# Linear attention on one core: sixteen heads per transfer, Q in 8 KB runs, and features computed one group ahead

## The chip, the cores and the metric

One core of one Trainium2 chip. The metric is the device time of one launch in microseconds. Ratios are the mean time of one kernel's fast runs over that of the other's of the same rounds, so they are not quite the ratio of the medians that are quoted beside them. "Span" is the profiled execution's own length; the timed figure of the same execution lies 1.7 to 2.0 us above it.

## The reference

```python
batch, heads, seq, dim = 8, 12, 512, 64          # Q, K, V: float32
Q_feat = np.maximum(0, Q) + 1
K_feat = np.maximum(0, K) + 1
KV = np.einsum('bhkd,bhkv->bhdv', K_feat, V)
K_sum = np.sum(K_feat, axis=2)
numerator = np.einsum('bhqd,bhdv->bhqv', Q_feat, KV)
denominator = np.einsum('bhqd,bhd->bhq', Q_feat, K_sum)
return numerator / (denominator[:, :, :, None] + 1e-10)
```

Each of Q, K, V and the output is 12.58 MB. There are 96 heads. The kernel handles them in twelve groups (0 to 11) of eight heads; two groups make a pair (0 to 5).

## The kernel before

Loads cast float32 to bf16 on the way and are issued by GpSimd (only the first K comes uncast, over SyncE). VectorE computes features, copies three quarters of V into a block layout and divides the outputs; ScalarE copies the last quarter of V, the transposed Q and the K·V matrices. TensorE does transposes, first matmuls (K·V) and output matmuls; the program keeps TensorE's results in PSUM tiles and all other tiles in the SBUF. The page's GB/s count a load after its cast: GpSimd's queue moved 28.84 MB, 10.49 of stores and 18.35 of loads, which is half of the 36.70 MB that these loads read.

```python
    def load(s, groups, names="kvq"):            # s: a pair
        ...
            nc.gpsimd.dma_start(
                out=t[:, ms], in_=drams[x][:, 2 * groups[0] : 2 * groups[-1] + 2]
            )                                    # rows of 16 x 64 floats: 4 KB runs
    def store(g):
        o_sb = outs.pop(g)
        o_to = o_dram[:, g * NP : g * NP + NP]
        if g < NG - 2:
            nc.gpsimd.dma_start(out=o_to, in_=o_sb)          # 1 MB
            return
        for h in range(2):
            nc.sync.dma_start(out=o_to[:, h:NP:2], in_=o_sb[:, h:NP:2])   # 512 KB
    def v_blocks(g):
        ...                                      # block 3 by nc.scalar.copy, 0 to 2 by nc.vector.tensor_copy
    def transposes(g):
        qf = qfs.pop(g)
        qt = mid_pool.tile([P, C, P, 2], BF16, name="qt")
        for half in range(2):
            qt_ps = psum_qt.tile([P, C, P], BF16, name="qt_ps")     # two buffers
            for c in range(C):
                nc.tensor.transpose(qt_ps[:, c, :], qf[:, half * C + c, :, :], identity)
            nc.scalar.copy(out=qt[:, :, :, half], in_=qt_ps)
        qts[g] = qt
    ...
        for g in range(NG - 1):
            k_features(g); v_blocks(g); q_features(g)     # joined on a line here
            if g:
                transposes(g - 1)
            if g >= 2:
                output(g - 2)
            keys_values(g)
            if g % 2 and g // 2 + 2 < NG // 2:
                load_pair(g // 2 + 2)
            if g >= LAG:
                store(g - LAG)                            # LAG = 3
        last = NG - 1
        k_features(last); v_blocks(last)
        transposes(last - 1)
        output(last - 2)
        q_features(last)
        keys_values(last)
        transposes(last)
        output(last - 1)
        output(last)
        for g in range(last - LAG, NG):
            store(g)
```

Of the kernel before, what the change touches and what calls it, by code (L numbers as in the profile page):

```python
# [8 lines left out]
FP32 = mybir.dt.float32  # L9
BF16 = mybir.dt.bfloat16  # L10
# [1 line left out]

BANK = 512
IN_BUFS = 2
OUT_BUFS = 6
LAG = 3


@with_exitstack
def kernel(  # L20
# [15 lines left out]



    nc = tc.nc

    B, H, S, D = Q.shape
    P = 128
    C = 8
    C2 = 2 * C
    NPAIR = B * H * S // (P * C)
    NP = 4
    NG = NPAIR // NP
    D1 = D + 1
    W = 2 * D1

    def view(t, c):
        return t.flatten_outer_dims().rearrange("(n p c) d -> p n c d", p=P, c=c)

    q_dram = view(Q, C2)
    k_dram = view(K, C2)
    v_dram = view(V, C2)
    o_dram = view(out, C)

    const = ctx.enter_context(tc.tile_pool(name="const", bufs=1))
    head_pool = ctx.enter_context(tc.tile_pool(name="head_pool", bufs=1))  # L60
    in_pool = ctx.enter_context(tc.tile_pool(name="in_pool", bufs=IN_BUFS))
    feat_pool = ctx.enter_context(tc.tile_pool(name="feat", bufs=2))
    mid_pool = ctx.enter_context(tc.tile_pool(name="mid", bufs=3))
    out_pool = ctx.enter_context(tc.tile_pool(name="out_pool", bufs=OUT_BUFS))
    recip_pool = ctx.enter_context(tc.tile_pool(name="recip", bufs=4))
    psum_kva = ctx.enter_context(tc.tile_pool(name="psum_kva", bufs=2, space=bass.MemoryType.PSUM))
# [1 line left out]
    psum_qt = ctx.enter_context(tc.tile_pool(name="psum_qt", bufs=2, space=bass.MemoryType.PSUM))  # L68

    identity = const.tile([P, P], BF16, name="identity")  # L70
# [4 lines left out]
    zero = const.tile([P, 1], FP32, name="zero")  # L75
    kva_diag = [const.tile([P, 4, 2, D1], BF16, name=f"kva_diag{i}") for i in range(NV)]

    drams = dict(k=k_dram, v=v_dram, q=q_dram)
    raw = {}
    kfs = {}  # L80
    qfs = {}
    qts = {}
    outs = {}

    def own(g):
        return slice(g % 2 * 2, g % 2 * 2 + 2)

    def load_first_k():
        k_raw = head_pool.tile([P, 2, C2, D], FP32, name="k_first")
        nc.sync.dma_start(out=k_raw, in_=k_dram[:, 0:2])  # L90
        raw["k", 0] = k_raw

    def load(s, groups, names="kvq"):
        ms = slice(groups[0] % 2 * 2, groups[-1] % 2 * 2 + 2)
        for x in names:
            if (x, "buf", s) not in raw:
                raw[x, "buf", s] = in_pool.tile([P, 4, C2, D], BF16, name=f"{x}_raw")
            t = raw[x, "buf", s]
            nc.gpsimd.dma_start(  # L99
                out=t[:, ms], in_=drams[x][:, 2 * groups[0] : 2 * groups[-1] + 2]  # L100
            )
            for g in groups:
                raw[x, g] = t[:, own(g)]

    def load_pair(s):
        if s < NG // 2 - 1:
            load(s, (2 * s, 2 * s + 1))
        else:
            load(s, (2 * s,))
            load(s, (2 * s + 1,))  # L110

    def store(g):
        o_sb = outs.pop(g)
        o_to = o_dram[:, g * NP : g * NP + NP]
        if g < NG - 2:
            nc.gpsimd.dma_start(out=o_to, in_=o_sb)  # L116
            return
        for h in range(2):
            nc.sync.dma_start(out=o_to[:, h:NP:2], in_=o_sb[:, h:NP:2])

    def feature(dst, src):
        nc.vector.tensor_scalar(  # L122
            out=dst, in0=src, scalar1=1.0, scalar2=1.0, op0=ALU.add, op1=ALU.max
        )

    def k_features(g):
        k_raw = raw.pop(("k", g))
        kf = feat_pool.tile([P, C2, 2, D], BF16, name="kf")
        for n in range(2):
            feature(kf[:, :, n], k_raw[:, n])  # L130
        kfs[g] = kf

    def v_blocks(g):
        v_raw = raw.pop(("v", g))
        for b in range(4):
            ps = slice(32 * b, 32 * b + 32)
            if b == 3:
                nc.scalar.copy(out=v_blk[g % 2][ps, b], in_=v_raw[ps])  # L138
            else:
                nc.vector.tensor_copy(out=v_blk[g % 2][ps, b], in_=v_raw[ps])  # L140

    def q_features(g):
        q_raw = raw.pop(("q", g))
        qf = feat_pool.tile([P, C2, 2, D], BF16, name="qf")
        for half in range(2):
            cs = slice(half * C, half * C + C)
            feature(qf[:, cs].rearrange("p c n d -> p n c d"), q_raw[:, :, cs])
        qfs[g] = qf

    def keys_values(g):  # L150
        kf = kfs.pop(g)
        sb = g % 2
        vb = v_all[:, 4 * sb : 4 * sb + 5]
        kva_ps = psum_kva.tile([P, 5, D], FP32, name="kva_ps")
        for c in range(C2):
            for n in range(2):
                nc.tensor.matmul(  # L157
                    kva_ps[64 * n : 64 * n + 64],
                    lhsT=kf[:, c, n, :],
                    rhs=vb[:, :, n, c, :],  # L160
                    start=(c == 0),
                    stop=(c == C2 - 1),
                )
        kva = kva_diag[g % NV]
        for n in range(2):
            ps = slice(64 * n, 64 * n + 64)
            nc.scalar.copy(out=kva[ps, :, n, 0:D], in_=kva_ps[ps, sb : sb + 4, :])  # L167
            nc.scalar.copy(out=kva[ps, :, n, D], in_=kva_ps[ps, 4 - 4 * sb, 0:4])  # L168

    def transposes(g):  # L170
        qf = qfs.pop(g)
        qt = mid_pool.tile([P, C, P, 2], BF16, name="qt")
        for half in range(2):
            qt_ps = psum_qt.tile([P, C, P], BF16, name="qt_ps")
            for c in range(C):
                nc.tensor.transpose(qt_ps[:, c, :], qf[:, half * C + c, :, :], identity)  # L176
            nc.scalar.copy(out=qt[:, :, :, half], in_=qt_ps)  # L177
        qts[g] = qt

    def output(g):  # L180
        kva = kva_diag[g % NV]
        qt = qts.pop(g)
        o_sb = out_pool.tile([P, NP, C, D], FP32, name="o_sb")
        for h in range(2):
            ops = [psum.tile([P, 2, BANK], FP32, tag="ps", name="o_ps") for _ in range(2)]
            for c in range(C):
                for j in range(2):
                    b = 2 * h + j
                    nc.tensor.matmul(  # L189
                        ops[c // 4][64 * j : 64 * j + 64, c // 2 % 2, (c % 2) * W : (c % 2) * W + W],  # L190
                        lhsT=qt[:, c, 32 * b : 32 * b + 32, :],
                        rhs=kva[:, b],
                        start=True,
                        stop=True,
                    )
            for i in range(2):
                cells = ops[i][:, :, 0 : 2 * W].rearrange("p b (c n x) -> p b c n x", n=2, x=D1)
                recip = recip_pool.tile([P, 2, 2, 2, 1], FP32, name="recip")
                nc.vector.reciprocal(out=recip, in_=cells[:, :, :, :, D:D1])  # L199
                nc.vector.tensor_tensor(  # L200
                    out=o_sb[:, h:NP:2, 4 * i : 4 * i + 4].rearrange(
                        "p n (b c) d -> p b c n d", b=2
                    ),
                    in0=cells[:, :, :, :, 0:D],
                    in1=recip.to_broadcast([P, 2, 2, 2, D]),
                    op=ALU.mult,
                )
        outs[g] = o_sb

    def clear(first, split, end):  # L210
        t = v_all.rearrange("p b m c d -> p (b m c d)").bitcast(FP32)
# [5 lines left out]

    with tc.manual_schedule():
        nc.gpsimd.memset(zero, 0.0)
        load_first_k()  # L220
        load(0, (0,), "vq")
        load(0, (1,))
        nc.vector.memset(ones, 0.0)
        for b in range(4):
            nc.vector.memset(ones[32 * b : 32 * b + 32, b : b + 1], 1.0)  # L225
        clear(0, 3, 5)
        e = v_all[:, 4, :, :, 0:4].rearrange("p n c j -> p (n c) j")
        nc.vector.tensor_copy(out=e, in_=ones[:, None, :].to_broadcast([P, 2 * C2, 4]))
        make_identity(nc, identity)
        for t in kva_diag:  # L230
            nc.gpsimd.memset(t, 0.0)  # L231
        load_pair(1)
        clear(5, 7, 9)
        for g in range(NG - 1):
            k_features(g)
            v_blocks(g)
            q_features(g)
            if g:
                transposes(g - 1)
            if g >= 2:  # L240
                output(g - 2)
            keys_values(g)
            if g % 2 and g // 2 + 2 < NG // 2:
                load_pair(g // 2 + 2)
            if g >= LAG:
                store(g - LAG)
        last = NG - 1
        k_features(last)
        v_blocks(last)
        transposes(last - 1)  # L250
        output(last - 2)
        q_features(last)
        keys_values(last)
        transposes(last)
        output(last - 1)
        output(last)
        for g in range(last - LAG, NG):
            store(g)


# [28 lines left out]
```

## Time and profile before

| | before |
|---|---|
| time, median | 127.14 us of 3 runs; 127.23 of 4 with the run beside the changed kernel |
| span of the profiled run | 125.8 us |
| busy: VectorE (DVE), ScalarE (ACT), TensorE (PE) | 88.2, 68.0, 65.2 us |
| transfers over the span | 400 GB/s, read and written together |
| transfers, packets under 512 B | 38, 608 |

No compute engine is busy for more than about 70% of the span, while the DMA row of the page is 9 from end to end (the prediction shows it). So read the DMA row first, and ask of each stage whether the transfers were kept fed; the average shares of the engines cannot say that.

### The profile page before, as it was taken

What the parts mean: (1) busy time and instruction counts of PE and PEld (TensorE: products, weight loads), DVE (VectorE), ACT (ScalarE), POOL (GpSimd) and SP (SyncE); (2) the same over time, 40 slices, a digit from 0 to 9 for tenths busy, and PEclk for the clock granted to TensorE, in tenths of its full rate; (3) what the DMA queues carried; (4) which work ended last, traced back from release to release, by engine and by line L of the source; (5) the groups of instructions that cost most, each with busy time, mean ns of one, the idle gap of its engine ahead of it and who ended that gap; (6) DMA issues with size and microseconds to landing.
All of it is one profiled execution on the core that took longest, in us unless ns stands there. A gap on an engine that the chain in (4) does not pass through costs nothing.

```text
span 125.8 us, 2337 instructions
## 1 busy us (share of the span) xinstructions
PE 65.2 (52%) x960; PEld 48.4 (39%) x960; DVE 88.2 (70%) x188; ACT 68.0 (54%) x87; POOL 27.8 (22%) x43
## 2 busy tenths in 40 slices
PE   0005939000059784796918476006978569694500
PEld 0003627000036564574806365004656447472300
DVE  4896280206199799999989990629959999758920
ACT  7832296006700889629892962750087971987000
POOL 6990213000002082023700260212221002020000
PEclk9999999755555999689999999955589976999955
DMA  3999999999999999999999999999999999999991
GB/s 76 341 211 209 210 213 211 210 212 211 212 211 212 211 214 212 210 212 214 253 414 287 209 210 212 213 369 380 209 210 210 211 287 418 418 417 410 403 391 72
DMA packets 13419, 32.13 MB, mean 255 GB/s; under 512 B 608, under 2 KB 608, under 8 KB 13408
## 3 DMA queue, kind: packets, MB, share of 16 engines
q0 software_dynamic: 12048, 28.84, 98.3%
q1 hardware_dynamic: 1360, 3.15, 6.8%
q8 instruction: 7, 0.11, 0.3%
q14 instruction: 4, 0.03, 0.1%
HBM read 37.75 MB, written 12.58 MB: 400 GB/s over the span
## 4 chain that ended last, share of the span: by engine, by line
DMA 40%; DVE 26%; PE 18%; POOL 6%; issue 6%; DVEq 0%; POOLq 0%
DMA q_raw<-in_Q_dram 40%; DVE o_sb L200 15%; PE kva_ps L157 11%; DVE v_all L140 4%; PE qt_ps L176 3%; DVE recip L199 3%; PE o_ps L189 3%; POOL v_raw L99 2%; DVE qf L122 2%; DVE kf L122 2%; POOL q_raw L99 1%; POOL kva_diag L231 1%; POOL k_raw L99 1%; POOL identity masks.py:199 0%; POOL identity masks.py:197 0%
## 5 line engine op out<-in xcount | busy, mean ns | idle before, releaser
L157 PE MATMUL kva_ps<-v_all,kf 128*64 128x320 bf16 x384 | 36.4, 356 | 13.1 <-DVE v_all L140 13.1
L189 PE MATMUL o_ps<-kva_diag,qt 128*64 128x130 bf16 x384 | 19.1, 234 | 40.9 <-DVE o_sb L200 40.4
L200 DVE TENSOR_TENSOR o_sb<-o_ps,recip 128x512 f32<-128x512 f32 x48 | 33.2, 692 | 1.6
L140 DVE COPY v_all<-v_raw 32x2048 bf16<-32x2048 bf16 x36 | 26.5, 736 | 10.9 <-DMA v_raw<-in_V_dram 10.6
L157 PEld LDWEIGHTS <-kf 128*64 128x64 bf16 x384 | 25.3, 133 | 20.9 <-DVE v_all L140 13.3
L189 PEld LDWEIGHTS <-qt 128*64 128x64 bf16 x384 | 12.7, 114 | 46.4 <-DVE o_sb L200 44.6
L138 ACT COPY v_all<-v_raw 32x2048 bf16<-32x2048 bf16 x12 | 22.7, 1894 | 13.3 <-DMA v_raw<-in_V_dram 13.1
L177 ACT COPY qt<-qt_ps 128x1024 bf16<-128x1024 bf16 x24 | 29.7, 1308 | 0.3
L167 ACT CAST kva_diag<-kva_ps 64x256 bf16<-64x256 f32 x24 | 8.9, 371 | 33.3 <-PE kva_ps L157 33.2
L122 DVE TENSOR_SCALAR qf<-q_raw 128x1024 bf16<-128x1024 bf16 x24 | 9.1, 423 | 6.6 <-DMA q_raw<-in_Q_dram 6.5
L99 POOL DMA_DIRECT2D k_raw<-in_K_dram x7 | 5.3, 754 | 38.1 <-DVE kf L122 37.3
L116 POOL DMA_DIRECT2D out_dram<-o_sb x10 | 8.4, 846 | 22.6 <-DVE o_sb L200 16.4
L176 PE MATMUL qt_ps<-identity,qf 128*128 128x128 bf16 x192 | 13.1, 222 | 0.0
L199 DVE RECIPROCAL recip<-o_ps 128x8 f32<-128x8 f32 x48 | 9.6, 199 | 4.9 <-PE o_ps L189 4.8
L122 DVE TENSOR_SCALAR kf<-k_raw 128x1024 bf16<-128x1024 bf16 x22 | 8.7, 437 | 6.0 <-DMA k_raw<-in_K_dram 6.0
L176 PEld LDWEIGHTS <-qf 128*128 128x128 bf16 x192 | 11.0, 99 | 3.3 <-issue 3.0
L99 POOL DMA_DIRECT2D v_raw<-in_V_dram x8 | 6.1, 764 | 18.8 <-ACT v_all L138 10.7
L99 POOL DMA_DIRECT2D q_raw<-in_Q_dram x8 | 5.9, 741 | 4.2 <-DMA q_raw<-in_Q_dram 4.2
L213 DVE MEMSET v_all<- 128x3072 f32 (+1 forms) x2 | 4.4, 2192 | 1.1 <-DVE ones L225 0.7
L168 ACT CAST kva_diag<-kva_ps 64x4 bf16<-64x4 f32 x24 | 4.0, 169 | 0.0
L214 ACT COPY v_all<-zero 128x2048 f32<-128x2048 f32 x2 | 3.7, 1894 | 0.0
L214 ACT ACT_TABLE_LOAD x1 | 1.3, 1283 | 0.7 <-PEq L273 0.7
(12 smaller groups left out, 4.6 us busy)
## 6 DMA issues: line engine op xcount, KB each, us to landing
out_dram<-o_sb POOLq DMA_DIRECT2D x10, 1024.0 KB, 20.2
k_raw<-in_K_dram POOLq DMA_DIRECT2D x4, 1024.0 KB, 18.0
v_raw<-in_V_dram POOLq DMA_DIRECT2D x4, 1024.0 KB, 20.9
q_raw<-in_Q_dram POOLq DMA_DIRECT2D x4, 1024.0 KB, 25.0
v_raw<-in_V_dram POOLq DMA_DIRECT2D x4, 512.0 KB, 17.3
q_raw<-in_Q_dram POOLq DMA_DIRECT2D x4, 512.0 KB, 17.1
out_dram<-o_sb SPq DMA_DIRECT2D x4, 512.0 KB, 5.1
k_raw<-in_K_dram POOLq DMA_DIRECT2D x3, 512.0 KB, 23.3
```

Source lines behind the costliest of these rows:

```text
L99: nc.gpsimd.dma_start(out=t[:, ms], in_=drams[x][:, 2 * groups[0] : 2 * groups[-1] + 2])
L116: nc.gpsimd.dma_start(out=o_to, in_=o_sb)
L122: nc.vector.tensor_scalar(out=dst, in0=src, scalar1=1.0, scalar2=1.0, op0=ALU.add, op1=ALU.max)
L138: nc.scalar.copy(out=v_blk[g % 2][ps, b], in_=v_raw[ps])
L140: nc.vector.tensor_copy(out=v_blk[g % 2][ps, b], in_=v_raw[ps])
L157: nc.tensor.matmul(kva_ps[64 * n : 64 * n + 64], lhsT=kf[:, c, n, :], rhs=vb[:, :, n, c, :], start=(c == 0), stop=(c == C2 - 1),)
L167: nc.scalar.copy(out=kva[ps, :, n, 0:D], in_=kva_ps[ps, sb : sb + 4, :])
L176: nc.tensor.transpose(qt_ps[:, c, :], qf[:, half * C + c, :, :], identity)
L177: nc.scalar.copy(out=qt[:, :, :, half], in_=qt_ps)
L189: nc.tensor.matmul(ops[c // 4][64 * j : 64 * j + 64, c // 2 % 2, (c % 2) * W : (c % 2) * W + W], lhsT=qt[:, c, 32 * b : 32 * b + 32, :], r ...
L199: nc.vector.reciprocal(out=recip, in_=cells[:, :, :, :, D:D1])
L200: nc.vector.tensor_tensor(out=o_sb[:, h:NP:2, 4 * i : 4 * i + 4].rearrange("p n (b c) d -> p b c n d", b=2), in0=cells[:, :, :, :, 0:D], i ...
```

## The change

Intent: fewer and larger transfers (a whole pair per load and per store), Q in 8 KB runs, which its transposes take four-way (the last pair in 4 KB runs, two-way), and features one group ahead of the matmuls. The diff, cut to its core:

```diff
-    def load_pair(s): ...
+    def load_q(s):
+        if s < NS - 1:
+            q_raw = in_pool.tile([P, 2, C4, D], BF16, name="q_raw")
+            nc.gpsimd.dma_start(out=q_raw, in_=q_dram[:, 2 * s : 2 * s + 2])   # 8 KB runs
+            rows = q_raw.rearrange("p n (r c) d -> p n r c d", c=C)
+            for e in range(2):
+                raw["q", 2 * s + e] = rows[:, :, :, 4 * e : 4 * e + 4]
+            return
+        ...                                     # last pair: 4 KB runs, in two loads
+    def store(s):
+        if s < NS - 1:
+            nc.gpsimd.dma_start(out=o_to, in_=o_sb)              # 2 MB
         else:
+            for i in range(4):
+                nc.sync.dma_start(out=o_to[:, i:8:4], in_=o_sb[:, i:8:4])   # 512 KB
     def transposes(g):
-            nc.scalar.copy(out=qt[:, :, :, half], in_=qt_ps)
+            nc.scalar.copy(
+                out=qts[g][:, lo : lo + CC // 2], in_=qt_ps.rearrange("p c r q -> p c q r")
+            )                    # one transposed tile per pair (R = 4), or per group (R = 2, last pair)
...
+        for g in range(last - 1):
+            k_features(g + 1)
+            v_blocks(g + 1)
+            if g + 1 < last - 1:
+                q_features(g + 1)
+            transposes(g)
+            keys_values(g)
             if g:
+                output(g - 1)
+            ...                  # store(s - 1) at odd g, loads of pair s + 2 at even g
         k_features(last)
         v_blocks(last)
+        keys_values(last - 1)
+        output(last - 2)
+        keys_values(last)
+        store(NS - 2)
+        q_features(last - 1)
         transposes(last - 1)
-        output(last - 2)
         q_features(last)
-        keys_values(last)
         transposes(last)
         output(last - 1)
         output(last)
+        store(NS - 1)
```

More of the change, by code (lines that the diff above doesn't have):

```diff
@@ L14 @@
 IN_BUFS = 2
-OUT_BUFS = 6
-LAG = 3
+OUT_BUFS = 3
 @with_exitstack
@@ L44 @@
     C2 = 2 * C
-    NPAIR = B * H * S // (P * C)
-    NP = 4
-    NG = NPAIR // NP
+    C4 = 4 * C
+    NS = B * H // 16
+    NG = 2 * NS
     D1 = D + 1
@@ L52, in view @@
         return t.flatten_outer_dims().rearrange("(n p c) d -> p n c d", p=P, c=c)
-    q_dram = view(Q, C2)
     k_dram = view(K, C2)
     v_dram = view(V, C2)
+    q_dram = view(Q, C4)
+    q_quad = view(Q, C2)
     o_dram = view(out, C)
@@ L62 @@
     feat_pool = ctx.enter_context(tc.tile_pool(name="feat", bufs=2))
-    mid_pool = ctx.enter_context(tc.tile_pool(name="mid", bufs=3))
+    mid_pool = ctx.enter_context(tc.tile_pool(name="mid", bufs=2))
     out_pool = ctx.enter_context(tc.tile_pool(name="out_pool", bufs=OUT_BUFS))
@@ L76 @@
     kva_diag = [const.tile([P, 4, 2, D1], BF16, name=f"kva_diag{i}") for i in range(NV)]
-    drams = dict(k=k_dram, v=v_dram, q=q_dram)
     raw = {}
@@ L83, with load_k @@
     outs = {}
-    def own(g):
-        return slice(g % 2 * 2, g % 2 * 2 + 2)
-    def load_first_k():
-        k_raw = head_pool.tile([P, 2, C2, D], FP32, name="k_first")
-        nc.sync.dma_start(out=k_raw, in_=k_dram[:, 0:2])
-        raw["k", 0] = k_raw
-    def load(s, groups, names="kvq"):
-        ms = slice(groups[0] % 2 * 2, groups[-1] % 2 * 2 + 2)
-        for x in names:
-            if (x, "buf", s) not in raw:
-                raw[x, "buf", s] = in_pool.tile([P, 4, C2, D], BF16, name=f"{x}_raw")
-            t = raw[x, "buf", s]
+    def load_k(s, es=(0, 1)):
+        if s == 0 and es == (0,):
+            k_raw = head_pool.tile([P, 2, C2, D], FP32, name="k_first")
+            nc.sync.dma_start(out=k_raw, in_=k_dram[:, 0:4:2])
+            raw["k", 0] = k_raw
+            return
+        k_raw = in_pool.tile([P, 4, C2, D], BF16, name="k_raw")
+        lo, step = es[0], 3 - len(es)
+        nc.gpsimd.dma_start(
+            out=k_raw[:, lo:4:step], in_=k_dram[:, 4 * s + lo : 4 * s + 4 : step]
+        )
+        for e in es:
+            raw["k", 2 * s + e] = k_raw[:, e:4:2]
@@ new lines, in load_v @@
+    def load_v(s):
+        v_raw = in_pool.tile([P, 4, C2, D], BF16, name="v_raw")
+        nc.gpsimd.dma_start(out=v_raw, in_=v_dram[:, 4 * s : 4 * s + 4])
+        for e in range(2):
+            raw["v", 2 * s + e] = v_raw[:, e:4:2]
+    def load_q(s):
[3 more added lines that the diff above has]
+            rows = q_raw.rearrange("p n (r c) d -> p n r c d", c=C)
+            for e in range(2):
+                raw["q", 2 * s + e] = rows[:, :, :, 4 * e : 4 * e + 4]
+            return
+        q_raw = in_pool.tile([P, 4, C2, D], BF16, name="q_raw")
+        rows = q_raw.rearrange("p n (r c) d -> p n r c d", c=C)
+        for e in range(2):
@@ L99, in load @@
             nc.gpsimd.dma_start(
-                out=t[:, ms], in_=drams[x][:, 2 * groups[0] : 2 * groups[-1] + 2]
+                out=q_raw[:, e:4:2], in_=q_quad[:, 4 * s + e : 4 * s + 4 : 2]
             )
-            for g in groups:
-                raw[x, g] = t[:, own(g)]
-    def load_pair(s):
-        if s < NG // 2 - 1:
-            load(s, (2 * s, 2 * s + 1))
-        else:
-            load(s, (2 * s,))
-            load(s, (2 * s + 1,))
-    def store(g):
-        o_sb = outs.pop(g)
-        o_to = o_dram[:, g * NP : g * NP + NP]
-        if g < NG - 2:
-            nc.gpsimd.dma_start(out=o_to, in_=o_sb)
-            return
-        for h in range(2):
-            nc.sync.dma_start(out=o_to[:, h:NP:2], in_=o_sb[:, h:NP:2])
+            raw["q", 2 * s + e] = rows[:, e:4:2]
@@ L121, in feature @@
+    def store(s):
+        o_sb = outs.pop(s)
+        o_to = o_dram[:, 8 * s : 8 * s + 8]
+        if s < NS - 1:
+            nc.gpsimd.dma_start(out=o_to, in_=o_sb)
+        else:
+            for i in range(4):
+                nc.sync.dma_start(out=o_to[:, i:8:4], in_=o_sb[:, i:8:4])
     def feature(dst, src):
@@ L143, in q_features @@
         q_raw = raw.pop(("q", g))
-        qf = feat_pool.tile([P, C2, 2, D], BF16, name="qf")
-        for half in range(2):
-            cs = slice(half * C, half * C + C)
-            feature(qf[:, cs].rearrange("p c n d -> p n c d"), q_raw[:, :, cs])
+        R, CC = q_raw.shape[2:4]
+        qf = feat_pool.tile([P, R, CC, 2, D], BF16, name="qf")
+        for n in range(2):
+            feature(qf[:, :, :, n], q_raw[:, n])
         qfs[g] = qf
@@ L171, in transposes @@
         qf = qfs.pop(g)
-        qt = mid_pool.tile([P, C, P, 2], BF16, name="qt")
-        for half in range(2):
-            qt_ps = psum_qt.tile([P, C, P], BF16, name="qt_ps")
-            for c in range(C):
-                nc.tensor.transpose(qt_ps[:, c, :], qf[:, half * C + c, :, :], identity)
-            nc.scalar.copy(out=qt[:, :, :, half], in_=qt_ps)
-        qts[g] = qt
+        R, CC = qf.shape[1:3]
+        if R == 2 or g % 2 == 0:
+            qts[g] = mid_pool.tile([P, C, P, R], BF16, name=f"qt{R}")
+        if R == 4 and g % 2:
+            qts[g] = qts[g - 1]
+        first = 0 if R == 2 else g % 2 * CC
+        for half in range(2):
+            qt_ps = psum_qt.tile([P, CC // 2, R, P], BF16, name="qt_ps")
+            for c in range(CC // 2):
+                for r in range(R):
+                    nc.tensor.transpose(
+                        qt_ps[:, c, r], qf[:, r, half * CC // 2 + c, :, :], identity
+                    )
+            lo = first + half * CC // 2
+            nc.scalar.copy(
+                out=qts[g][:, lo : lo + CC // 2], in_=qt_ps.rearrange("p c r q -> p c q r")
+            )
     def output(g):
+        s, e = g // 2, g % 2
         kva = kva_diag[g % NV]
-        qt = qts.pop(g)
-        o_sb = out_pool.tile([P, NP, C, D], FP32, name="o_sb")
+        qt = qts[g]
+        R = qt.shape[3]
+        if e == 0:
+            outs[s] = out_pool.tile([P, 8, C, D], FP32, name="o_sb")
+        o_sb = outs[s]
         for h in range(2):
@@ L188, in output @@
                     b = 2 * h + j
+                    q = 16 * (4 * e + b) if R == 4 else 32 * b
                     nc.tensor.matmul(
                         ops[c // 4][64 * j : 64 * j + 64, c // 2 % 2, (c % 2) * W : (c % 2) * W + W],
-                        lhsT=qt[:, c, 32 * b : 32 * b + 32, :],
+                        lhsT=qt[:, c, q : q + 64 // R, :],
                         rhs=kva[:, b],
@@ L200, in output @@
                 nc.vector.tensor_tensor(
-                    out=o_sb[:, h:NP:2, 4 * i : 4 * i + 4].rearrange(
+                    out=o_sb[:, 2 * e + h : 8 : 4, 4 * i : 4 * i + 4].rearrange(
                         "p n (b c) d -> p b c n d", b=2
@@ L207, in output @@
                 )
-        outs[g] = o_sb
     def clear(first, split, end):
@@ L219 @@
         nc.gpsimd.memset(zero, 0.0)
-        load_first_k()
-        load(0, (0,), "vq")
-        load(0, (1,))
+        load_k(0, (0,))
+        load_v(0)
+        load_q(0)
+        load_k(0, (1,))
         nc.vector.memset(ones, 0.0)
@@ L231 @@
             nc.gpsimd.memset(t, 0.0)
-        load_pair(1)
+        load_k(1)
+        load_v(1)
+        load_q(1)
         clear(5, 7, 9)
-        for g in range(NG - 1):
-            k_features(g)
-            v_blocks(g)
-            q_features(g)
-            if g:
-                transposes(g - 1)
-            if g >= 2:
-                output(g - 2)
-            keys_values(g)
-            if g % 2 and g // 2 + 2 < NG // 2:
-                load_pair(g // 2 + 2)
-            if g >= LAG:
-                store(g - LAG)
-        last = NG - 1
+        last = NG - 1
+        k_features(0)
+        v_blocks(0)
+        q_features(0)
+        for g in range(last - 1):
[5 more added lines that the diff above has]
+            keys_values(g)
+            if g:
+                output(g - 1)
+            s = g // 2
+            if g % 2 and s >= 1:
+                store(s - 1)
+            elif g % 2 == 0 and s + 2 < NS:
+                load_k(s + 2)
+                load_v(s + 2)
+                load_q(s + 2)
         k_features(last)
         v_blocks(last)
+        keys_values(last - 1)
[3 more added lines that the diff above has]
+        q_features(last - 1)
         transposes(last - 1)
-        output(last - 2)
         q_features(last)
-        keys_values(last)
         transposes(last)
@@ L256 @@
         output(last)
-        for g in range(last - LAG, NG):
-            store(g)
+        store(NS - 1)
 _INS = ['Q', 'K', 'V']
```

## The prediction

> **What bounds the kernel now.** I read the page first (parts 2 and 4), then the windows, then the engines' timelines in order of time from 78 us to the end. Part 2 says that the DMA engines are never idle between the first slice and the last; a load casts, so 210 GB/s written to the SBUF are 420 GB/s read.
>
> ```profile
> DVE  4896280206199799999989990629959999758920
> DMA  3999999999999999999999999999999999999991
> GB/s 76 341 211 209 210 213 211 210 212 211 212 211 212 211 214 212 210 212 214 253 414 287 209 210 212 213 369 380 209 210 210 211 287 418 418 417 410 403 391 72
> ```
>
> The reader is to see an unbroken row of 9s, and only two levels in the rates: about 211 (loads) and about 415 (stores). The windows give the levels exactly (last number GB/s, before it the DMA share):
>
> ```profile
> 20.00:30.00 10.00, 1.81 (x36) 1.38 (x32) 1.45 (x4) 1.71 (x6) 0.00 (x0) 0.69 1.12 212
> 105.00:110.00 5.00, 3.77 (x66) 2.82 (x64) 3.77 (x9) 3.54 (x6) 0.00 (x0) 0.93 1.02 418
> ```
>
> So 37.75 MB read at 422 take 89.4 us and 12.58 MB written at 417 take 30.2 us: 119.6 us of the 125.8. The rest is the start (first bytes near 2 us, full rate near 3) and the end. The end is where the change acts, so here are VectorE (DVE) in the last 22 us and the group before:
>
> ```profile
> 79.17 2.15 DVE L140 COPY v_all<-v_raw 32x2048 bf16<-32x2048 bf16 x3 [3.43 <-DMA v_raw<-in_V_dram]
> 84.10 0.76 DVE L122 TENSOR_SCALAR qf<-q_raw 128x1024 bf16<-128x1024 bf16 x2 [2.77 <-DMA q_raw<-in_Q_dram]
> ...
> 103.63 0.75 DVE L122 TENSOR_SCALAR kf<-k_raw 128x1024 bf16<-128x1024 bf16 x2
> 104.30 2.35 DVE L140 COPY v_all<-v_raw 32x2048 bf16<-32x2048 bf16 x3
> 107.74 0.21 DVE L199 RECIPROCAL recip<-o_ps 128x8 f32<-128x8 f32 x1 [1.10 <-PE o_ps L189]
> ...
> 111.11 0.75 DVE L122 TENSOR_SCALAR qf<-q_raw 128x1024 bf16<-128x1024 bf16 x2
> 113.55 0.21 DVE L199 RECIPROCAL recip<-o_ps 128x8 f32<-128x8 f32 x1 [1.69 <-PE o_ps L189]
> ...
> 119.67 0.69 DVE L200 TENSOR_TENSOR o_sb<-o_ps,recip 128x512 f32<-128x512 f32 x1
> ```
>
> VectorE finishes the last output at 120.36; half-microsecond windows show the DMA at its full 400 GB/s until 122.5 and trickling out by 124.4. Thus DMA bounds the kernel, but VectorE's last output has only about 2 us to spare: the last store is issued behind a backlog of about 1 us of earlier ones.
>
> [...]this is ScalarE (ACT), whose transposed-Q copies had long been ready and start only when the copy of V ahead of them is done:
>
> ```profile
> 79.23 1.89 ACT L138 COPY v_all<-v_raw 32x2048 bf16<-32x2048 bf16 x1 [2.26 <-DMA v_raw<-in_V_dram]
> 81.14 2.45 ACT L177 COPY qt<-qt_ps 128x1024 bf16<-128x1024 bf16 x2
> ```
>
> [...]the same 32 matmuls take 4.01 us after a quiet stretch and 2.34 after a busy one.
>
> ```profile
> 102.34 4.01 PE L157 MATMUL kva_ps<-v_all,kf 128*64 128x320 bf16 x32
> 109.82 2.34 PE L157 MATMUL kva_ps<-v_all,kf 128*64 128x320 bf16 x32
> ```
>
> **The change part by part.** Call the six pairs of groups 0 to 5 and the twelve groups 0 to 11.
>
> *Transfers.* Bytes are the same. Q of pairs 0 to 4 (10.5 MB) goes in 8 KB instead of 4 KB runs: 1280 packets fewer[...]. Transfers fall from 38 to 29; the page's 608 packets under 512 B are 16 per transfer[...]. [...] The order in the single GpSimd queue is kept: loads 0 to 3, one pair's worth of stores, load 4, another, load 5, the rest. So the bytes ahead of the last Q are the same. Before, that Q lands near 104.0 (84.10 for Q of pair 4, then two stores at 2.52 and six half loads at 2.48). After: 103.5. V of pair 5 now comes as one transfer with only Q's 4.97 us behind it, so it lands at 98.5.
>
> *Loop.* With Q in 8 KB runs, transposes of an even group fill columns 0 to 3 of the shared transposed tile and those of the odd group 4 to 7, and output reads all eight. So output of an even group now waits for the transposes of the next, odd, one. That is why features run one group ahead. Walking through VectorE's order with 3.8 us of features and 3.4 us of output per group, it waits for Q of pair 4 until about 84.4, finishes output 7 at about 95.6, and has 2 us of slack when V lands at 98.5. Buffers come free 10 us and more before their next load must start, so I expect no gap in the DMA until the end.
>
> *The end*, from V at 98.5, each duration from the rows shown:
> - ScalarE: V block 1.9, then two copies of transposes 9, 2.5: 103.0. Only then can columns 4 to 7 of output 8 be multiplied. VectorE: V blocks until 100.7, one quarter of output 8, idle from 101.6 to 103.25, three more quarters at 0.845: 105.9. Stall of 1.7.
> - K features and V blocks of group 11, 3.0: 108.9. Output 9, whose matmuls stand behind the first matmuls of group 10 (cold, 104.7 to 108.7): 109.1 to 112.5.
> - Q features 10 and 11: 114.0. TensorE: first matmuls of group 11 from 111.2 to 113.5 (2.1 after output began, as at 107.74 and 109.82 before), then transposes 10. ScalarE: 1.1 for K·V of group 11 until 114.7, copies of transposes 10 until 117.2. There are two transpose buffers, so the second half of transposes 11 runs at 117.2 to 117.7, and output 10 stands behind it in TensorE's order: first result 118.1. **VectorE is idle from 114.0 to 118.1.** Before, transposes 10 were done far earlier and this gap was 1.69.
> - Outputs 10 and 11: 6.8 (113.55 to 120.36 before): **124.9**, against 120.36: 4.5 later.
> - The earlier stores end by about 119.3, so the last 512 KB finds the queue empty. It saves the backlog of 1.2 us. Span: 125.8 + 4.5 - 1.2 = 129.1[...]. The timed runs are 1.34 above the profiled span (127.14 - 125.8): 130.2. I take **129.9**, shaded a little toward the rival below.
>
> **Rivals.** *DMA stays the bound to the end.* If V came two or three us earlier or the two stalls were shorter, the end would be the old one less the 0.5 of the DMA: 126.6. For it: everything up to 104 is DMA-bound and the change is tuned to it. Against: the two stalls follow from the order and from measured durations, and VectorE had only 2 us to spare; 4.5 is more than that. *The first stall vanishes, the second stays.* If the group 10 matmuls run warm or ScalarE's copies are quicker with the four-way layout, 1.7 us come off: 128.2 to 128.5. *It is worse:* the four-way strided read of PSUM by ScalarE, or the features' four-way writes, may take longer than the 1.24 and 0.42 us now shown; one group more late at the end would add 1 to 2 us: 131.5. [...]
>
> **Range and chances.** The arrival of V is good to 0.5 us, the chain of 26.4 us after it to about 1.5, mostly downward by the first stall, and the last store's lone latency to 0.7. This gives 127.5 to 131.6 for 8 in 10. Slower by over 2% begins at 129.68, just under my sum, so it is little better than even: 0.53. Within 2%: 0.44. Faster by over 2% (under 124.6)[...]: 0.03.
>
> **What would show it.** Right: DMA at its two levels without a gap until about 113, then windows falling below 300 GB/s between 119 and the end; V of pair 5 waited for by VectorE and ScalarE at 98 to 99; VectorE idle about 1.7 us in the middle of output 8, and about 4 us ahead of output 10, released by TensorE's output matmuls; last output at 124 to 126; the chain of waits ending in the copies of transposes and first matmuls of the last groups. Step wrong: feature or copy rows with other mean durations; load windows above 215 GB/s (8 KB runs worth more); the transpose gap under 2 us. The whole would be wrong if the DMA still ran at 400 GB/s up to 2 us before the end: then the end has slack that I do not see, and the time is 126.6.

Both terms of the transfers' gain came to 0.5 us, an estimate: it makes 103.5 of 104.0 for the last Q, and so 98.5 for V of pair 5, and it is in the rival's 126.6. A further term of 0.2 us took the span from 129.1 to 128.9, and with the 1.34 above the span the sum came to 130.2. Measured: the two copies of Q at 81.14 had their transposes done at 77.04, and ScalarE, idle for 2.26 us until 79.23, first ran the copy of V. Of the two rows of 32 matmuls, TensorE's granted clock was 0.58 over that of 4.01 us ("cold" in the prediction) and 1.00 over that of 2.34 ("warm"); its longest wait between the transposes before each and the row itself was 2.06 and 0.81 us. What sets the clock is not shown.

## The result, and the profile after

The changed kernel takes 130.49 us (median of 4, 130.35 to 130.93) against 127.23; ratio 1.0253, 95% interval 1.0216 to 1.0291: slower by over 2%. Its span is 128.6 us.

The rows of part 2 of the changed kernel's page, to be laid beside those of before:

```profile
DVE  4953239306299996999989972379691859972980
DMA  3999999999999999999999999999999999949884
GB/s 104 298 191 214 210 212 213 213 214 220 203 212 215 217 212 210 210 217 214 321 397 227 196 212 220 259 417 283 206 212 216 226 397 422 401 173 378 335 317 180
```

Up to slice 35 of 40 the DMA is as full as before, at the same two levels. Then there is a hole (4, 173 GB/s) and one more full slice, and after that it reaches no 9. So the DMA loses its time in the last 16 us. VectorE from the landing of the last V on (start, duration, what, and in brackets the idle time before it with what ended it):

```profile
99.95 2.08 DVE L150 COPY v_all<-v_raw 32x2048 bf16<-32x2048 bf16 x3 [2.98 <-DMA v_raw<-in_V_dram]
...
104.37 0.21 DVE L224 RECIPROCAL recip<-o_ps 128x8 f32<-128x8 f32 x1 [1.38 <-PE o_ps L214]
...
113.04 1.82 DVE L132 TENSOR_SCALAR qf<-q_raw 128x1024 bf16<-128x1024 bf16 x4
118.09 0.21 DVE L224 RECIPROCAL recip<-o_ps 128x8 f32<-128x8 f32 x1 [3.23 <-PE o_ps L214]
...
124.21 0.69 DVE L225 TENSOR_TENSOR o_sb<-o_ps,recip 128x512 f32<-128x512 f32 x1
```

V of the last pair lands at 99.95; VectorE then stalls twice for output matmuls, 1.38 us inside output 8 and 3.23 us ahead of output 10, and ends at 124.90, 4.5 us later than before. What held TensorE back is in ScalarE's and TensorE's timelines:

```profile
100.00 1.89 ACT L148 COPY v_all<-v_raw 32x2048 bf16<-32x2048 bf16 x1 [6.49 <-DMA v_raw<-in_V_dram]
101.92 1.93 ACT L196 COPY qt<-qt_ps 128x1024 bf16<-128x1024 bf16 x2
...
115.12 3.76 ACT L196 COPY qt<-qt_ps 128x1024 bf16<-128x1024 bf16 x4
```

```profile
95.02 1.07 PE L192 MATMUL qt_ps<-identity,qf 128*128 128x128 bf16 x16
...
103.90 0.86 PE L214 MATMUL o_ps<-kva_diag,qt 128*64 128x130 bf16 x12 [0.49 <-ACT qt L196]
...
114.02 1.07 PE L192 MATMUL qt_ps<-identity,qf 128*128 128x128 bf16 x16
116.18 0.61 PE L192 MATMUL qt_ps<-identity,qf 128*128 128x128 bf16 x8 [1.09 <-ACT qt L196]
117.09 0.61 PE L192 MATMUL qt_ps<-identity,qf 128*128 128x128 bf16 x8 [0.31 <-ACT qt L196]
117.63 0.64 PE L214 MATMUL o_ps<-kva_diag,qt 128*64 128x130 bf16 x16
```

First stall: the transposes of group 9 were in PSUM at 96.1, ScalarE was idle for 6.49 us, and yet their copies ran only at 101.9, since in ScalarE's order they stand behind a copy of V that had not landed. Second stall: the transposes of group 10 are done at 115.1, and ScalarE copies them from 115.12 to 117.05 (the first two of the line's four copies); output 10 needs these copies. In addition the transposes of group 11 wait twice for a free transpose buffer (1.09 and 0.31 us), and output 10, which does not need them, stands behind them until 117.63: that is the last 0.6 us of the stall.

### The profile page after: what moved, and what is told of

Read it like the earlier page. It is cut to its first block, busy times and chain, and to the rows that moved or that the text cites. A ratio compares the mean times of both kernels' runs of the same rounds, so it can differ in the third digit from the quotient of the medians.

```text
span 128.6 us, 2330 instructions
## 1 busy us (share of the span) xinstructions
PE 69.0 (54%) x960; PEld 52.1 (41%) x960; DVE 88.3 (69%) x188; ACT 60.8 (47%) x87; POOL 21.8 (17%) x34
## 4 chain that ended last, share of the span: by engine, by line
DMA 55%; DVE 23%; PE 8%; ACT 4%; issue 4%; POOL 2%; POOLq 0%; ACTq 0%
DMA v_raw<-in_V_dram 22%; DMA q_raw<-in_Q_dram 21%; DMA k_raw<-in_K_dram 12%; DVE o_sb L225 12%; DVE v_all L150 5%; PE kva_ps L167 5%; ACT qt L196 3%; DVE recip L224 3%; PE qt_ps L192 2%; DVE kf L132 2%; PE o_ps L214 1%; ACT v_all L148 1%; POOL v_raw L102 1%; DVE qf L132 1%; POOL q_raw L109 1%
## 5 line engine op out<-in xcount | busy, mean ns | idle before, releaser
L214 PE MATMUL o_ps<-kva_diag,qt 128*64 128x130 bf16 x384 | 21.2, 243 | 36.3 <-DVE o_sb L225 19.9
L167 PE MATMUL kva_ps<-v_all,kf 128*64 128x320 bf16 x384 | 34.8, 345 | 0.0
L214 PEld LDWEIGHTS <-qt 128*64 128x64 bf16 x384 | 14.3, 119 | 42.7 <-DVE o_sb L225 24.0
L196 ACT COPY qt<-qt_ps 128x1024 bf16<-128x1024 bf16 x24 | 23.0, 1016 | 10.1 <-PE qt_ps L192 10.0
L192 PE MATMUL qt_ps<-identity,qf 128*128 128x128 bf16 x192 | 16.4, 252 | 18.6 <-DVE qf L132 17.2
L192 PEld LDWEIGHTS <-qf 128*128 128x128 bf16 x192 | 13.9, 114 | 20.3 <-DVE qf L132 17.4
L126 POOL DMA_DIRECT2D out_dram<-o_sb x5 | 5.6, 1117 | 42.5 <-DVE o_sb L225 42.5
L102 POOL DMA_DIRECT2D v_raw<-in_V_dram x6 | 4.6, 770 | 7.4 <-issue 3.9
L109 POOL DMA_DIRECT2D q_raw<-in_Q_dram x5 | 3.6, 712 | 0.0
L132 DVE TENSOR_SCALAR kf<-k_first 128x1024 bf16<-128x1024 f32 x2 | 1.6, 860 | 0.0
```

Source lines behind the costliest of these rows:

```text
L102: nc.gpsimd.dma_start(out=v_raw, in_=v_dram[:, 4 * s : 4 * s + 4])
L132: nc.vector.tensor_scalar(out=dst, in0=src, scalar1=1.0, scalar2=1.0, op0=ALU.add, op1=ALU.max)
L167: nc.tensor.matmul(kva_ps[64 * n : 64 * n + 64], lhsT=kf[:, c, n, :], rhs=vb[:, :, n, c, :], start=(c == 0), stop=(c == C2 - 1),)
L192: nc.tensor.transpose(qt_ps[:, c, r], qf[:, r, half * CC // 2 + c, :, :], identity)
L196: nc.scalar.copy(out=qts[g][:, lo : lo + CC // 2], in_=qt_ps.rearrange("p c r q -> p c q r"))
L214: nc.tensor.matmul(ops[c // 4][64 * j : 64 * j + 64, c // 2 % 2, (c % 2) * W : (c % 2) * W + W], lhsT=qt[:, c, q : q + 64 // R, :], rhs=kv ...
```

## The experiments

All ten gave correct results. "The loss" below is the 3.3 us between the two medians. Runs of one call shared a chip and the runs of the kernel before; its median was 127.79 in the first call (the first four experiments), 127.32 in the second (the next four), 127.18 in the third. One caution for all timelines: V of the last pair landed at 99.0 to 100.3 us in the nine profiled executions whose loads come in the changed kernel's order, so ends of outputs are best compared from that landing on. In the changed kernel the last output ends 24.95 us after it.

### Fill the hole alone (e1_fill_gap)

```diff
             if g % 2 and s >= 1:
                 store(s - 1)
+            if g == last - 2:
+                store_half(NS - 2, 0)     # two 512 KB stores: group 8
...
-        store(NS - 2)
+        store_half(NS - 2, 1)             # two 512 KB stores: group 9
```

> The changed kernel with one thing different: the stores of pair 4 are issued in quarters of 512 KB, those of group 8 as soon as output 8 is done (about 107) and those of group 9 after output 9. This fills the DMA's hole that the changed kernel's profile shows between 112 and 115 (1.8 to 2.3 us of lost transfer time). Chain theory (the end is set by VectorE's last output and the last quarter's store behind it): the hole goes, the last output stays at 124.9, the time stays at 130.4 within 0.4. Rival (the time lost is transfer time lost in that hole): 128.3, about 2 us faster.

Measured: 130.80 us, ratio to the kernel before 1.0233 (1.0183 to 1.0282), so no better than the changed kernel; the last output is at 125.3. Windows of this run (in each: length, busy time of PE, PEld, DVE, ACT, POOL with instruction counts, granted clock, DMA share, GB/s), first of the changed kernel, then of this one:

```profile
112.00:115.00 3.00, 3.00 (x48) 2.46 (x43) 2.82 (x7) 0.79 (x4) 0.89 (x1) 1.00 0.38 149
117.00:120.00 3.00, 1.68 (x34) 1.25 (x35) 1.82 (x5) 1.88 (x3) 0.00 (x0) 1.00 1.02 378
```

```profile
112.00:115.00 3.00, 3.00 (x52) 2.43 (x47) 2.96 (x7) 0.48 (x3) 1.43 (x2) 1.00 1.05 422
117.00:120.00 3.00, 1.69 (x34) 1.17 (x31) 1.53 (x4) 2.18 (x3) 0.00 (x0) 1.00 0.41 167
```

The hole is filled (0.38 becomes 1.05) and comes back five microseconds later, where the transfers wait for outputs. In the changed kernel lost transfer time is not what sets the end: VectorE's last output is.

### Remove the first stall (e2_copies_first)

```diff
+            if g == last - 2:
+                transposes(g)
             v_blocks(g + 1)
             if g + 1 < last - 1:
                 q_features(g + 1)
-            transposes(g)
+            if g < last - 2:
+                transposes(g)
```

> The changed kernel with one thing different: in the iteration of group 9 the transposes of group 9 and their copies by ScalarE are issued ahead of the V copy of group 10, so they no longer stand behind the arrival of V. Chain theory: the stall of 1.38 us inside output 8 goes; output 8 ends near 105.4 in place of 107.0, and the first result of output 9 comes at 108.3 to 108.6 if the first matmuls of group 10 (cold, 3.6 to 4.0 us, from about 104.2) do not hold it longer; last output near 123.6, time 129.2. If those matmuls hold output 9, less: 129.8. Rival (transfers set the end): no change, 130.4.

Measured: 129.38 us, ratio 1.0127 (1.0091 to 1.0162), 1.1% below the run that filled the hole, in the same rounds. The stall inside output 8 is gone and that output ends at 105.5 in place of 107.0. Of the 1.5 us, VectorE gives 1.11 back at once, waiting for output 9 behind the first matmuls of group 10, as the expectation had allowed:

```profile
109.24 0.21 DVE L224 RECIPROCAL recip<-o_ps 128x8 f32<-128x8 f32 x1 [1.11 <-PE o_ps L214]
```

In the profiled run the last output comes at 124.56, only 0.3 us earlier (24.6 us after V); that run was the slowest of the four (130.01 us). So the stall's mechanism is shown, and a gain of 1.1 us by the medians, of which the profiled run shows only part.

### Remove the second stall (e3_early_t10)

```diff
+        q_features(last - 1)
         k_features(last)
         v_blocks(last)
         keys_values(last - 1)
+        transposes(last - 1)
         output(last - 2)
+        q_features(last)
         keys_values(last)
         store(NS - 2)
-        q_features(last - 1)
-        transposes(last - 1)
-        q_features(last)
         transposes(last)
```

> The changed kernel with one thing different: at the end the Q features of group 10 come ahead of the K features of group 11, and the transposes of group 10 ahead of output 9, so that only one group's transposes are left ahead of output 10. Chain theory: VectorE's stall ahead of output 10 falls from 3.23 us to 1.5 to 1.8, the last output from 124.9 to 123.2, the time from 130.5 to 128.8. Rival (transfers set the end): no change, 130.4.

Measured: 130.48 us, ratio 1.0228 (1.0176 to 1.0279): no gain that these runs can tell from none. Yet the stall did shrink as expected, from 3.23 to 1.69 us, and the last output came at 124.2 although V had landed 0.4 later (23.9 us after V):

```profile
117.38 0.21 DVE L224 RECIPROCAL recip<-o_ps 128x8 f32<-128x8 f32 x1 [1.69 <-PE o_ps L214]
```

The gain went into a new limit. The windows of this run (its profiled execution was the slowest of the four, 131.75 us; the others took 130.21 to 130.65):

```profile
112.00:115.00 3.00, 2.02 (x36) 1.65 (x38) 2.90 (x8) 1.07 (x2) 0.00 (x0) 1.00 0.34 138
115.00:117.00 2.00, 2.00 (x34) 1.54 (x30) 0.70 (x3) 0.88 (x4) 0.89 (x1) 1.00 0.08 33
117.00:120.00 3.00, 1.40 (x32) 0.91 (x32) 2.51 (x7) 1.93 (x2) 0.00 (x0) 1.00 1.01 371
123.00:126.00 3.00, 0.00 (x0) 0.00 (x0) 1.16 (x3) 0.00 (x0) 0.00 (x0) 0.54 1.04 387
126.00:128.00 2.00, 0.00 (x0) 0.00 (x0) 0.00 (x0) 0.00 (x0) 0.00 (x0) 0.50 0.94 356
```

The added work ahead of output 9 delayed that output, and with it the 2 MB store of pair 4, from 113.42 in the changed kernel to 115.32 (0.4 of these 1.9 us is V's later landing). The hole now lasts until about 117. From there 4.2 MB remain (pair 4 and pair 5), and at some 387 GB/s they take 10.8 us: 127.8, which is where the DMA falls silent. Between 117 and 128 it is full. So a second limit lay close behind VectorE's last output: what is still to be transferred after the hole.

### Both stalls (e4_both)

> Both of the two reorderings together. Chain theory: the gains add up, about 2.9 us: last output near 122.0, time 127.6, so nearly all of the change's loss of 3.3 is given back, and the kernel is again within 0.5% of the one before. Rival (one stall only hides the other): no better than the better one of the two.

The edit is the two above together. Measured: 129.08 us, ratio 1.0112 (1.0064 to 1.0161), so about half of the loss is given back in place of nearly all. The last output is at 121.4 (122.0 expected), but 0.9 us of that is V's earlier landing, at 99.01. From V on it takes 22.4 us, 2.6 less than in the changed kernel, where the repairs alone gave 0.3 and 1.1. One profiled execution each, so this only suggests that each stall hides part of the other. And the hole between 112 and 114 remains, while the DMA is full from there until 125. By now the second limit holds.

### Both stalls and the hole (e5_both_filled)

> e4_both and e1_fill_gap together: the changed kernel with both reorderings and with the stores of pair 4 in quarters, those of group 8 issued right after output 8. Theory as it stands after the first four runs: two limits lie close behind each other at the end, VectorE's last output (with its lone last store) and the transfers still to be done behind the DMA's hole; each of the earlier runs moved one of them alone. Together: last output near 121.2 as in e4_both, no hole at 112 to 114, transfers done near 123.3, time 127.2 (1.9 us under e4_both's 129.08), even with the kernel before. Rival (the hole costs nothing, as e1_fill_gap alone suggested, and e4_both was held by something else): 129.1.

The edit is the first three together. Measured: 128.07 us, ratio 1.0060 (1.0007 to 1.0113). The distance to the kernel before fell from 1.1% with both stalls alone to 0.6%; the two intervals overlap, so the times by themselves only suggest a gain. The traces say more: the DMA's share between 112 and 115 goes from 0.58 (both stalls, first line) to 1.03 (this run), and its last activity from 125 to 124.

```profile
112.00:115.00 3.00, 2.78 (x50) 2.12 (x46) 1.28 (x5) 1.65 (x5) 0.89 (x1) 1.00 0.58 228
112.00:115.00 3.00, 3.00 (x54) 2.35 (x50) 1.31 (x4) 1.38 (x5) 0.72 (x1) 1.00 1.03 414
```

Filling the hole moved nothing while VectorE's last output stood behind it, and by the traces moves the end once that output is earlier. The expected 127.2 was not reached: the last output ended at 121.8, and windows from 117 on show the DMA at 0.91 and 0.82, still short of outputs.

### Q in 4 KB runs everywhere (e6_quads)

```diff
-            q_raw = in_pool.tile([P, 2, C4, D], BF16, name="q_raw")
-            nc.gpsimd.dma_start(out=q_raw, in_=q_dram[:, 2 * s : 2 * s + 2])
+            q_raw = in_pool.tile([P, 4, C2, D], BF16, name="q_raw")
+            nc.gpsimd.dma_start(out=q_raw, in_=q_quad[:, 4 * s : 4 * s + 4])
...
```

> e5_both_filled with Q of all pairs read in 4 KB runs, one transfer per pair (the changed kernel's layout for its last pair). The end is transfer-bound in e5_both_filled by the theory, so this weighs the 8 KB runs by themselves. [...]this is 0.3 us slower than e5_both_filled. Rival (8 KB runs are worth nothing): no difference beyond 0.2 us. [...]

The 0.3 us was the estimate; what it was worked out from is not shown by any trace.

Measured, on top of the three repairs: 128.53 us, 0.5 above the same kernel with 8 KB runs, on the same chip, but the intervals of the two ratios overlap (1.0078, 1.0036 to 1.0119), and outputs end later here (123.0), so the time does not weigh the runs cleanly. The landings do. VectorE waits for both V and Q of pair 4, and Q follows V in the queue. Its timeline in the changed kernel, then in this run:

```profile
79.48 2.08 DVE L150 COPY v_all<-v_raw 32x2048 bf16<-32x2048 bf16 x3 [3.23 <-DMA v_raw<-in_V_dram]
84.34 0.76 DVE L132 TENSOR_SCALAR qf<-q_raw 128x1024 bf16<-128x1024 bf16 x2 [2.79 <-DMA q_raw<-in_Q_dram]
```

```profile
80.09 2.08 DVE L155 COPY v_all<-v_raw 32x2048 bf16<-32x2048 bf16 x3 [3.17 <-DMA v_raw<-in_V_dram]
85.01 0.76 DVE L137 TENSOR_SCALAR qf<-q_raw 128x1024 bf16<-128x1024 bf16 x2 [2.84 <-DMA q_raw<-in_Q_dram]
```

The distance is 4.86 us with 8 KB runs, and 4.86 to 4.88 in the five experiments above that have them; it is 4.92 here, and 4.93 in the kernel before (79.17 to 84.10 in the prediction's lines). Of the four runs below, the two with 4 KB runs agree (4.94, 4.95), and of the two with 8 KB runs one does (4.87) and one does not (5.01, the last run). An 8 KB Q load is thus about 0.07 us shorter, in seven executions of eight; for five loads that would be 0.35 us.

### The kernel before, its last outputs made earlier (e7_before_interleaved)

```diff
-    def output(g):
+    def output(g, between=None):
         for h in range(2):
+            if h and between is not None:
+                transposes(between)
...
-        transposes(last - 1)
-        output(last - 2)
+        output(last - 2, between=last - 1)
         q_features(last)
         keys_values(last)
-        transposes(last)
-        output(last - 1)
+        output(last - 1, between=last)
```

> The kernel before with the transposes of groups 10 and 11 moved between the first and second half of the output matmuls of groups 9 and 10, so that VectorE no longer waits for them. Last output near 118.7 in place of 120.4. If the end of the kernel before is set by how late its last store is issued: 126.3 to 126.7. If it is set by the transfers alone[...]: 127.2, no change.

Measured: 127.73 us, ratio 1.0024 (0.9973 to 1.0075): no change. The last output came at 119.0 in place of 120.4 and bought nothing; the DMA's last windows are full until 122 as before (the kernel before, then this run):

```profile
121.00:122.00 1.00, 0.00 (x0) 0.00 (x0) 0.00 (x0) 0.00 (x0) 0.00 (x0) 0.50 0.96 373
121.00:122.00 1.00, 0.00 (x0) 0.00 (x0) 0.00 (x0) 0.00 (x0) 0.00 (x0) 0.50 1.02 395
118.33 0.69 DVE L202 TENSOR_TENSOR o_sb<-o_ps,recip 128x512 f32<-128x512 f32 x1
```

The kernel before is bound by its transfers up to the end, as the prediction had it.

### The copy layout alone, in the kernel before (e8_before_copies)

```diff
-            qt_ps = psum_qt.tile([P, C, P], BF16, name="qt_ps")
...
-            nc.scalar.copy(out=qt[:, :, :, half], in_=qt_ps)
+            qt_ps = psum_qt.tile([P, C // 2, 2, P], BF16, name="qt_ps")
...
+            nc.scalar.copy(
+                out=qt[:, lo : lo + C // 2], in_=qt_ps.rearrange("p c r q -> p c q r")
+            )
```

> The kernel before with one part of the change alone: the transposes are laid out in PSUM so that ScalarE's copies write the transposed Q contiguously and read it in steps, in place of reading contiguously and writing every other element. Expected: the copies' mean falls from 1.31 to about 1.0 us, as in the changed kernel; ScalarE isn't on the path, so the time stays at 127.2 to 127.8 within 0.3. Rival (ScalarE's shorter copies move the end): 0.3 to 0.8 us faster.

Measured: 127.19 us, ratio 0.9982 (0.9934 to 1.0030): the time stays. The copies' row of part 5, in the kernel before and in this run (busy time in us, mean of one in ns):

```profile
L177 ACT COPY qt<-qt_ps 128x1024 bf16<-128x1024 bf16 x24 | 29.7, 1308 | 0.3
```

```profile
L181 ACT COPY qt<-qt_ps 128x1024 bf16<-128x1024 bf16 x24 | 23.1, 1015 | 0.3
```

One part of the change is a real gain of 0.29 us per copy (1308 to 1015 ns), 6.6 us of ScalarE over the kernel, with nothing on the path to spend it on. Only this net was measured, not the stepped reading and the contiguous writing apart.

### All three repairs and the interleaving (e9_interleaved)

> e5_both_filled with the transposes of groups 10 and 11 between the halves of outputs 9 and 10, as in e7_before_interleaved. In e5_both_filled the windows from 116 on still show the DMA at 0.77 to 0.94 in the last stretch, waiting for outputs that end at 121.8. Last output here near 119. Theory (both limits at the end are moved out of the way, so only the transfers are left, and 8 KB runs give them 0.35 us less than the kernel before has): 126.9, that is 0.3% under the kernel before, which five rounds may not resolve. Rival (the larger transfers themselves cost something that no order gives back): no better than e5_both_filled, 128.0.

The edit is that of both stalls and the hole, with the interleaving shown two sections above. Measured: 127.73 us, ratio 1.0041 (1.0013 to 1.0068). The last output is at 119.9 and the DMA is full until 122, as in the kernel before:

```profile
119.25 0.69 DVE L232 TENSOR_TENSOR o_sb<-o_ps,recip 128x512 f32<-128x512 f32 x1
121.00:122.00 1.00, 0.00 (x0) 0.00 (x0) 0.00 (x0) 0.00 (x0) 0.00 (x0) 0.50 1.05 406
```

So the end is mended. The 0.4% that remain are small but clear of noise, and they go against the theory, which asked for 0.3% under the kernel before. Where the 8 KB runs' 0.35 us and this remainder of 0.5 us go is not settled. The rival of the expectation stays open: no run changes only the size of the transfers, and by time this run is not clear of the one without the interleaving (1.0060; the intervals overlap). The traces give one hint, at the start: in the third of the 40 slices (about 6.3 to 9.6 us) the changed kernel, this run and the next, with the changed order of loads, show 191, 198 and 203 GB/s, the kernel before and its interleaved version 211 and 209.

### The last stores on GpSimd's queue (e10_last_pool)

```diff
-                nc.sync.dma_start(out=o_to[:, i:8:4], in_=o_sb[:, i:8:4])
+                nc.gpsimd.dma_start(out=o_to[:, i:8:4], in_=o_sb[:, i:8:4])
```

> e9_interleaved with the last four stores on GpSimd's queue in place of SyncE's. Windows with SyncE's stores show 385 to 400 GB/s, those with GpSimd's alone 418, over the last 7 us: 0.3 us to be had; against it, each issue takes GpSimd 0.72 us. Expected 0.1 to 0.3 us under e9_interleaved if the rate is the queue's; 0.3 us or more over it if the issue and the first byte are later.

Measured: 128.33 us, ratio 1.0107 (1.0071 to 1.0143), 0.6 us over the run before it on the same chip. Nothing shows the lower rate at the end to be a property of SyncE's queue: the windows between 117 and 120 show 381 to 389 GB/s here too.

No version tried beats the kernel before.

## Why the prediction was right

- **Time.** Forecast 129.9 with 127.5 to 131.6, slower with 0.53; measured 130.49, slower. The sum before its shading was 130.2: the shading went the wrong way. Its step from span to time (1.34 us) sets the median against the span of another execution: the profiled one took 127.54, 1.74 over its span.
- **What bounds before.** Transfers, with 2 us to spare for VectorE's last output. Shown: ending it 1.3 us earlier (119.0 in place of 120.4) left the time alone.
- **8 KB runs.** The 0.5 us for fewer packets and fewer transfers was an estimate that no trace showed. By landings, 8 KB runs gave 0.35 us (an estimate: five times the 0.07 of one load). The nine fewer transfers are weighed by no run alone, and a gain from them was not seen; in the end the DMA gained nothing that the time shows.
- **V of the last pair.** 98.5 forecast, 99.95 measured, the largest miss of a term. About 0.8 of the 1.45 us lie in the forecast's own sum: Q of pair 4 was to land at 84.4 by its walk through the loop and did so at 84.34, and with a pair's store (5.04) and two loads (4.97 each) V then comes at 99.3. The 98.5 counted on a gain of the transfers that was not there. The other 0.6 us is within the spread: that same stretch, from Q of pair 4 to V of pair 5, took 14.9 to 16.5 us over the nine profiled executions with this order. In both kernels the rate takes some 1 to 2 us from 102 on to climb from the loads' level to the stores' (half-microsecond windows from 101.5 on: 209, 299, 315, 393 GB/s before; 217, 258, 295, 344, 397 after). What makes it climb so slowly and the landings scatter is not shown.
- **First stall.** 1.7 forecast, 1.38 measured. Its mechanism was shown by the run that moved the copies.
- **Second stall.** 4.1 forecast, 3.2 measured. Order as forecast. VectorE came to it 0.9 us later than forecast (114.9 for 114.0, after the late V), yet output 10 began as forecast, at 118.09 (118.1). The term that was mis-sized, here and in the first stall, is ScalarE's copies, taken from the kernel before: two take 2.45 us there and 1.93 after. The change's layout makes them shorter. The prediction had this only among its rivals: as a gain that would remove the whole first stall, which it did not, and the other way round as a loss. (The features' four-way writes, feared there too, took 439 ns in place of 423.)
- **Last output.** 124.9 forecast, 124.90 measured: V was later and the stalls shorter by nearly the same amount, so the exact hit is partly luck.
- **The lone last store.** 4.0 to 4.2 us from last output to end of span forecast, 3.7 measured.
- **What it missed.** It expected the DMA "without a gap until about 113" and then only low windows near the end. The hole at 112 to 115 was real, and its consequence is that a second limit stands right behind the first. The stalls' account of the loss is true for the changed kernel as it stands, but it does not say what removing them is worth: removing the second alone gained nothing that the time shows, and removing both gave back about half.

## What to carry to other kernels

When a kernel's transfers are full, ask of each change only what it does to the last few microseconds: when the last big load lands, which engine's order of work stands between it and the last store, and whether stores are at hand in small enough pieces to fill the wait (here a 2 MB store that waited for all its outputs left the DMA at a share of 0.38 for 3 us). A copy that the program puts behind the copy of a load still under way waited for that load, though its own data were ready (here transposes done at 96.1, copied only at 101.9). And when a repair that shortens a wait brings nothing, look for the limit right behind it before calling the theory wrong: here two limits had to be moved together.
